# Modulation rows of the first feed-forward stage tied behind evacuations and handed out by products done

## The chip, the core and the metric

The kernel runs on one core of a Trainium2 chip. The metric is the device time of one execution in microseconds, the median of three runs. Engines are named as in the profile: PE is TensorE (matrix products; PEld are its weight loads), DVE is VectorE, ACT is ScalarE, POOL is GpSimd, and SP is the engine whose queue starts most of the DMA transfers. Every engine runs its own instructions strictly in the order in which they stand in its queue.

## What is computed

Two transformer layers run one after the other on 512 tokens of width 1024. The first ends with a feed-forward block; the second begins by scaling and shifting its input with a modulation vector that depends on nothing but the input `c`. Cut to that:

```python
# end of the first layer (D_FF = 2816)
h2 = rms_norm(x, g_ffn)
x = x + (silu(h2 @ w_gate) * (h2 @ w_up)) @ w_down
# second layer
mod = silu(c) @ w_mod + b_mod                  # 1024 x 6144 matrix, one vector of 6 * 1024
sh1, sc1, g1, sh2, sc2, g2 = split(mod, 6)
h = _rms(x, norm1_w) * (1 + sc1) + sh1
...                                            # projections, S5 scan, windowed attention, x += g1 * (...)
h2 = _rms(x, norm2_w) * (1 + sc2) + sh2
x = x + g2 * conv_ffn(h2)                      # second feed-forward block, same sizes
```

Everything is float32; a matrix product is made of three products of a high and a low part (high by high, high by low, low by high).

## The kernel before

**Products.** Each weight piece of 1024 x 128 (512 KB) is loaded as `raw` on SP's queue (two buffers). ACT copies it into `whi`, and DVE subtracts to get `wlo` (`whi` and `wlo` have five buffers each). A piece feeds 24 products of 128x512, three for each of eight slices. In the second feed-forward block `wlo` is made by ACT and an accumulating DMA on POOL's queue instead (`w8`), for the up weights.

**The feed-forward stages.** `ffn` runs over six chunks of hidden blocks (2, 4, 4, 4, 4, 4 blocks of 128). `up(c)` makes each hidden block from 48 products into two PSUM banks. In the first stage `hidden1` evacuates them: DVE writes `fg` from the gate bank, ACT applies silu, DVE writes `fu` from the up bank, multiplies, and `split` writes `hd`, the high part on ACT and the low part on DVE. `down(c)` makes eight output blocks from 3 products for each hidden block of the chunk, so 6 or 12, and DVE adds each bank into `x` (`down1`). The order is up(0), up(1), down(0), up(2), down(1), and so on; that is 1056 products for the hidden blocks and 528 for the outputs. The banks of the first stage come from a ring of three called `acc`. The last four output blocks are done apart, by halves of 256 tokens (`norm_tail`), and then `start_u` needs the modulation vector to begin the second layer.

**The modulation.** `modulation` makes the vector in rows of 128 numbers: 40 rows in the first feed-forward stage (`modT`), 8 in the second (`modG`). A row is two transfers of 256 KB into `wm` (three buffers, SP's queue) and two vector products on DVE (`CUSTOM_DVE_ANT_0` in the trace, `ISA wm,mh<-wm,cb` in the order; each is followed by a short read of the accumulator into `mh`). It is a generator: `ffn` calls `after()` behind every hidden block and every output block, `fill` then lets each of its two generators run one step further, and a row takes one or two such steps by turns. The other generator, `s5_tables`, makes tables for the second layer on DVE and POOL, with a few products and transposes on PE.

**What sets the order.** The code gives the order in which instructions are traced; a scheduler then orders each engine's queue and may move an instruction ahead of those traced before it, as soon as its operands and buffers would be there by the scheduler's own estimate. What a queue's head waits for holds everything behind it.

Of the kernel before, what the change touches and what calls it, by code (L numbers as in the profile page):

```python
# [38 lines left out]
B2 = 1  # L39
# [18 lines left out]
QK = 12  # L58
ORDER1 = "K0 TA KX0 K1 KX1 Q0 A0 QX0 Q1 dq0 A1 dq1 B QX1 QX2 CC QX3 ns00 ns01 dk0 dqx0 CD CS CT pq0 dkx0 ns10 dv0 dv1 dv2 ns11 dv3 ns20 nv00 nv01 nv10 ns30 nv11 ns21 nv20 dk1 dqx1 ns31 dkx1 nv21 nv30 TD ds0 nv31 pk0 pq1 ds1 ds2 dw0 ds3 dw1 dw2 F0 pv0 F1 pv1 dw3 F6 ss12 pv2 ss01 ss00 pv3 pk1 ss21 c0 ss32 ss31 ss13 c1 ss02 ss23 ss03 ss20 ss11 c2 ss22 F7 ss10 sv00 sv01 sv02 sv03 sv10 ss30 sv11 sv12 sv13 sv20 sv21 c3 c4 sv22 M0 ss33 c5 sv23 M1 F2 sv30 sv31 F4 sv32 sv33 F3 F5"
MOD1 = 40  # L60
EARLY = (0, 1, 6, 7, 2, 3)
LATE = (4, 5)

# [168 lines left out]
def build(tc, I, out, PV, PVN, CS, CSN, CS1, CSN1):  # L232
# [263 lines left out]

    def split(dst, src):
        act(dst[:, 0], src, AF.Copy)
        V.tensor_tensor(dst[:, 1], src, dst.bitcast(F32)[:, 0], op=ALU.subtract)  # L499

    def rsqrt_(o, ms, scale=1.0):

# [550 lines left out]
    d_x = dpool.tile([KD, P, S], F32, name="d_x")  # L1053
    d_z = [dpool.tile([8, 16, 8, 64], F32, name=f"d_z{q}") for q in range(4)]

    modG = cpool.tile([P, 8], F32, name="modG")

    def modulation(pool, j0, j1, dst, wait):

        n_ = j1 - j0  # L1060
        cb = pool.tile([P, D], F32, name="cb")
        nc.sync.dma_start(cb, I["cbc"])
        act(cb, cb, AF.Silu)
        mh = pool.tile([P, 2, n_], F32, name="mh")
        yield
        for j in range(n_):
            for n in range(2):
                wm = pool.tile([P, 512], F32, tag="wm", bufs=3, name="wm")
                nc.sync.dma_start(wm, I["wmod"][j0 + j][:, n * 512:(n + 1) * 512])
                V.tensor_tensor_reduce(wm, wm, cb[:, n * 512:(n + 1) * 512], 1.0, 0.0, ALU.mult, ALU.add, mh[:, n, j:j + 1])  # L1070
            for _ in range(wait(j)):
                yield
        V.tensor_tensor(dst, mh[:, 0], mh[:, 1], op=ALU.add)
        V.tensor_tensor(dst, dst, V1("b_mod")[:, j0:j1], op=ALU.add)
        yield
# [153 lines left out]
            nc.gpsimd.dma_start(d_rot[q], rt.rearrange("p b g c -> p b (g c)"))  # L1229
            yield  # L1230

    fillers = [s5_tables(), modulation(s5p, 0, MOD1, modT, lambda j: 1 + j % 2)]

    def fill():
        for f in fillers:
            next(f, None)

    def ffn(wn_up, wn_down, hin, hidden, add_down, after=lambda: None, start=None, tail=None, banks=(acc,)):
        banks = itertools.cycle(banks)
        hid = {}  # L1240
        started = {} if start is None else start

        def up(c):
            r, n = FCH[c]
            for j in range(r // 2, (r + n) // 2):
                ws = weights(wn_up, 2 * j), weights(wn_up, 2 * j + 1)
                for m in range(2):
                    ps = []
                    for a in range(2):
                        p_ = started.pop((j, m, a), None)  # L1250
                        if p_ is None:
                            p_ = next(banks)()
                            proj_f(p_, ws[a], hin, m)
                        ps.append(p_)
                    hid[2 * j + m] = hidden(2 * j + m, *ps)
                    after()

        def down(c):
            r, n = FCH[c]
            last = c == len(FCH) - 1  # L1260
            for k in range(8 if not (last and tail) else 8 - TAIL):
                ps = next(banks)()
                proj_f(ps, weights(wn_down, 4 * c + k // 2), hid, k % 2, k0=r)
                add_down(k, ps, last)
                after()
            if last and tail:
                tail(lambda k, ps, cs: proj_f(ps, weights(wn_down, 4 * c + k // 2), hid, k % 2, k0=r, cs=cs), add_down)

        up(0)
        for c in range(1, len(FCH)):  # L1270
            up(c)
            down(c - 1)
        down(len(FCH) - 1)
# [32 lines left out]
    def hidden1(j, pg, pu):  # L1306
        t = ftile("fg")
        V.scalar_tensor_tensor(t, pg, -0.5, r2, op0=ALU.mult, op1=ALU.mult)
        last_silu[0] = act(t, t, AF.Silu)
        u = ftile("fu")  # L1310
        V.scalar_tensor_tensor(u, pu, -0.5, r2, op0=ALU.mult, op1=ALU.mult)
        V.tensor_tensor(u, u, t, op=ALU.mult)  # L1312
        hd = hidp.tile([P, 2, S], F32R, tag="hid", name="hd")
        split(hd, u)
        return hd

    tot = sumtile()
# [11 lines left out]
    sq7 = fp.tile([P, S], F32, name="sq7")  # L1329

    def down1(k, ps, last, cs=ALL):
        V.tensor_tensor(x[k][:, cs], x[k][:, cs], ps[:, cs], op=ALU.add)  # L1332
        if last:
            dbg(f"x3_{k}", x[k])
            nc.gpsimd.dma_start(d_x[k][:, cs], x[k][:, cs])
# [371 lines left out]
    def hidden2(j, pval, pgate):  # L1707
# [2 lines left out]
        act(b, b, AF.Silu)  # L1710
        V.tensor_tensor(a, a, b, op=ALU.mult)
        hd = hidp.tile([P, 2, S], F32R, tag="hid", name="hd")
        split(hd, a)
        return hd

    def down2(k, ps, last):
# [1 line left out]
        if last:  # L1718
            nc.sync.dma_start(out[k * P:(k + 1) * P, :], x[k])

    last8 = modulation(fp, MOD1, 48, modG, lambda j: j % 2)
    ffn("w8", "w9", h2, hidden2, down2, lambda: next(last8, None), start=started, banks=(tr, sc, acc) if B2 else (acc,))
    ff.close()
    st.close()

# [25 lines left out]
```

## Time and profile before

| What | Value |
|---|---|
| Median of three runs | 1324.84 us (1318.99 to 1326.08) |
| The profiled execution, its own time | 1322.45 us |
| Its span in the trace | 1320.6 us |
| PE busy | 1238.6 us, 94% of the span |
| PE weight loads busy | 995.6 us, 75% |
| DVE busy | 835.3 us, 63% |
| ACT busy | 553.1 us, 42% |
| POOL busy | 319.4 us, 24% |
| Mean DMA rate | 146 GB/s |

PE is the busiest engine, so a change is worth what it takes from PE's idle time or from products done at a low clock. The first feed-forward stage lies at about 315 to 712 us of the span, the second from about 945 us to the end. The granted clock of PE is given in a trace as a share of full speed, 2.4 GHz; the lower of its two levels is half of that.

### The profile page before, as it was taken

What the parts mean: (1) busy time and instruction counts of PE and PEld (TensorE: products, weight loads), DVE (VectorE), ACT (ScalarE), POOL (GpSimd) and SP (SyncE); (2) the same over time, 40 slices, a digit from 0 to 9 for tenths busy, and PEclk for the clock granted to TensorE, in tenths of its full rate; (3) what the DMA queues carried; (4) which work ended last, traced back from release to release, by engine and by line L of the source; (5) the groups of instructions that cost most, each with busy time, mean ns of one, the idle gap of its engine ahead of it and who ended that gap; (6) DMA issues with size and microseconds to landing.
All of it is one profiled execution on the core that took longest, in us unless ns stands there. A gap on an engine that the chain in (4) does not pass through costs nothing.

```text
span 1320.6 us, 17314 instructions
## 1 busy us (share of the span) xinstructions
PE 1238.6 (94%) x6269; PEld 995.6 (75%) x6269; DVE 835.3 (63%) x1617; ACT 553.1 (42%) x917; POOL 319.4 (24%) x403
## 2 busy tenths in 40 slices
PE   6999999999988979999999977979889999999998
PEld 5888765667867758888888977758867788888887
DVE  7667868777977988554446588665746353434362
ACT  5434466445212213232233334665645544444430
POOL 3000004012417439391411142023121312121200
PEclk9999999999998999999999997789989999999999
DMA  6531111126567675534435883367498979595921
GB/s 214 147 118 48 49 32 49 48 80 197 152 214 221 215 243 156 160 121 126 132 105 177 274 195 103 99 162 139 97 224 187 225 161 189 126 192 120 192 88 64
DMA packets 211014, 192.96 MB, mean 146 GB/s; under 512 B 13041, under 2 KB 173697, under 8 KB 210929
## 3 DMA queue, kind: packets, MB, share of 16 engines
q1 hardware_dynamic: 154384, 146.96, 36.7%
q0 software_dynamic: 51456, 40.61, 19.3%
q10 hardware_dynamic: 5088, 4.29, 1.0%
q8 instruction: 50, 0.82, 0.3%
q14 instruction: 36, 0.29, 0.1%
HBM read 178.22 MB, written 15.43 MB: 147 GB/s over the span
## 4 chain that ended last, share of the span: by engine, by line
PE 56%; DVE 10%; DMA 8%; issue 5%; ACT 2%; POOL 1%; SPq 0%; DVEq 0%; POOLq 0%; ACTq 0%
PE acc L260 37%; PE sc L260 10%; PE tr L260 8%; DMA wm<-in_wmod_dram 4%; DVE wm L1070 2%; DMA wlo<-in_w_dram 2%; DMA raw<-in_w_dram 2%; DVE wlo L372 2%; PE po L260 1%; PE tr L1600 0%; POOL wlo L370 0%; DVE fu L1312 0%; ACT whi L366 0%; DVE x L1332 0%; DVE hd L499 0%
## 5 line engine op out<-in xcount | busy, mean ns | idle before, releaser
L260 PE MATMUL acc<-hl,whi 128*128 128x512 f32 (+1 forms) x1624 | 485.6, 382 | 15.9 <-ACT whi L366 7.5
L260 PEld LDWEIGHTS acc<-hl,whi 128*128 128x128 f32 x1624 | 296.2, 190 | 83.6 <-issue 14.0
L366 ACT ACTIVATE whi<-raw 128x1024 fp32r<-128x1024 f32 (+1 forms) x187 | 194.0, 1039 | 378.0 <-PE acc L260 193.9
L260 PE MATMUL acc<-hl,wlo 128*128 128x512 f32 (+1 forms) x812 | 309.0, 381 | 1.0 <-DMA wlo<-in_w_dram 1.0
L372 DVE TENSOR_TENSOR wlo<-raw,whi 128x1024 fp32r<-128x1024 f32 (+1 forms) x133 | 174.1, 1311 | 62.1 <-ACT whi L366 59.3
L260 PEld LDWEIGHTS acc<-hl,wlo 128*128 128x128 f32 x812 | 153.6, 189 | 33.7 <-issue 3.2
L260 PE MATMUL acc<-hd,whi 128*128 128x512 f32 (+1 forms) x472 | 147.8, 396 | 17.1 <-DVE x L1332 9.4
L370 POOL DMA_DIRECT2D wlo<-in_w_dram x54 | 72.0, 1334 | 328.1 <-ACT wlo L369 240.7
L260 PEld LDWEIGHTS acc<-hd,whi 128*128 128x128 f32 x472 | 88.7, 193 | 40.3 <-DVE x L1332 9.6
L260 PE MATMUL acc<-whi,hl 128*128 128x256 f32 (+1 forms) x544 | 111.4, 296 | 3.8 <-DVE v L249 2.2
L1070 DVE CUSTOM_DVE_ANT_0 wm<-wm,cb 128x512 f32<-128x512 f32 x96 | 79.8, 846 | 49.3 <-DMA wm<-in_wmod_dram 42.5
L260 PEld LDWEIGHTS acc<-whi,hl 128*128 128x128 f32 x544 | 91.2, 200 | 8.6 <-ACT tok L247 3.0
L260 PE MATMUL acc<-hd,wlo 128*128 128x512 f32 (+1 forms) x236 | 93.1, 394 | 0.0
L260 PE MATMUL acc<-wlo,hl 128*128 128x256 f32 (+1 forms) x272 | 80.0, 294 | 0.5 <-DVE wlo L372 0.5
L260 PE MATMUL tr<-hl,whi 128*128 128x512 f32 (+1 forms) x240 | 74.1, 392 | 0.0
L260 PE MATMUL sc<-hl,whi 128*128 128x512 f32 x208 | 64.9, 393 | 0.0
L369 ACT ACTIVATE wlo<-raw 128x1024 fp32r<-128x1024 f32 x54 | 56.5, 1046 | 3.9 <-PE acc L260 2.0
L260 PEld LDWEIGHTS acc<-wlo,hl 128*128 128x128 f32 x272 | 54.3, 200 | 2.5 <-DVE wlo L372 1.0
L919 POOL TENSOR_SCALAR_AFFINE_SELECT keep<-keep 128x128 f32<-128x128 f32 x16 | 9.3, 596 | 186.6 <-ACT keep L913 185.8
L260 PE MATMUL tr<-hl,wlo 128*128 128x512 f32 (+1 forms) x120 | 47.2, 394 | 7.4 <-DMA wlo<-in_w_dram 7.4
L260 PEld LDWEIGHTS acc<-hd,wlo 128*128 128x128 f32 x236 | 45.6, 193 | 10.0
L1332 DVE TENSOR_TENSOR x<-x,acc 128x512 f32<-128x512 f32 (+1 forms) x49 | 32.0, 655 | 33.0 <-PE acc L260 33.0
(424 smaller groups left out, 1960.1 us busy)
## 6 DMA issues: line engine op xcount, KB each, us to landing
raw<-in_w_dram SPq DMA_DIRECT2D x177, 512.0 KB, 4.4
wlo<-in_w_dram POOLq DMA_DIRECT2D x54, 512.0 KB, 8.0
wm<-in_wmod_dram SPq DMA_DIRECT2D x96, 256.0 KB, 4.1
xk<-in_xT_dram SPq DMA_DIRECT2D x16, 256.0 KB, 4.9
d_g<-s5g POOLq DMA_DIRECT2D x4, 576.0 KB, 4.1
gt<-d_g SPq DMA_DIRECT2D x4, 576.0 KB, 5.4
w1c<-in_w1k_dram SPq DMA_DIRECT2D x8, 256.0 KB, 5.7
w1c<-in_w1v_dram SPq DMA_DIRECT2D x8, 256.0 KB, 6.1
```

Of the source, the lines that this page charges most:

```text
L260: nc.tensor.matmul(o, lhsT=l, rhs=r, start=start, stop=stop, **k)
L366: act(hi[:, :m], raw[:, :m], AF.Copy)
L369: act(lo[:, :m], raw[:, :m], AF.Copy, scale=-1.0)
L370: nc.gpsimd.dma_start(v(lo), self.src[:, k0:k1, c0:c1], accum_op=ALU.add)
L372: V.tensor_tensor(lo[:, :m], raw[:, :m], hi.bitcast(F32)[:, :m], op=ALU.subtract)
L919: G.affine_select(g[:, d], g[:, d], fill=1.0, **past)
L1070: V.tensor_tensor_reduce(wm, wm, cb[:, n * 512:(n + 1) * 512], 1.0, 0.0, ALU.mult, ALU.add, mh[:, n, j:j + 1])
L1332: V.tensor_tensor(x[k][:, cs], x[k][:, cs], ps[:, cs], op=ALU.add)
```

## The change

Three things change in how the modulation rows are handed out.

- Each vector product is traced inside `tc.issue_after(done[0].ins)`. It must then stand behind that instruction in DVE's queue. `done[0]` is the last evacuation step traced so far: the DVE half of `split` for a hidden block (`hidden1`, `hidden2`), or the addition into `x` (`down1`). The tie is an order within one queue and makes no semaphore. The `wm` transfers are not tied.
- `fill` counts products. A hidden block adds 48 and an output block `3 * n`, times `MOD_RATE` = 0.0275; a whole credit runs the modulation one step. So a row comes every 36 products. `s5_tables` still gets one step for each call.
- In the second stage the eight rows are handed out at two steps for each call, instead of two rows for every two calls.

```diff
+MOD_RATE = 0.0275
...
-        V.tensor_tensor(dst[:, 1], src, dst.bitcast(F32)[:, 0], op=ALU.subtract)
+        return V.tensor_tensor(dst[:, 1], src, dst.bitcast(F32)[:, 0], op=ALU.subtract)
...
+    done = [None]
...
-                V.tensor_tensor_reduce(wm, wm, cb[:, n * 512:(n + 1) * 512], 1.0, 0.0, ALU.mult, ALU.add, mh[:, n, j:j + 1])
-            for _ in range(wait(j)):
-                yield
+                with tc.issue_after(done[0].ins) if done[0] is not None else nullcontext():
+                    V.tensor_tensor_reduce(wm, wm, cb[:, n * 512:(n + 1) * 512], 1.0, 0.0, ALU.mult, ALU.add, mh[:, n, j:j + 1])
+            yield
...
-    fillers = [s5_tables(), modulation(s5p, 0, MOD1, modT, lambda j: 1 + j % 2)]
+    fillers = [s5_tables(), modulation(s5p, 0, MOD1, modT)]
+    credit = [1.0]
 
-    def fill():
-        for f in fillers:
-            next(f, None)
+    def fill(products):
+
+        next(fillers[0], None)
+        credit[0] += products * MOD_RATE
+        while credit[0] >= 1.0:
+            credit[0] -= 1.0
+            next(fillers[1], None)
...
-                    after()
+                    after(6 * KD)
...
-                after()
+                after(3 * n)
...
-        split(hd, u)
+        done[0] = split(hd, u)
...
-        V.tensor_tensor(x[k][:, cs], x[k][:, cs], ps[:, cs], op=ALU.add)
+        done[0] = V.tensor_tensor(x[k][:, cs], x[k][:, cs], ps[:, cs], op=ALU.add)
...
-        split(hd, a)
+        done[0] = split(hd, a)
...
-    last8 = modulation(fp, MOD1, 48, modG, lambda j: j % 2)
-    ffn("w8", "w9", h2, hidden2, down2, lambda: next(last8, None), start=started, banks=(tr, sc, acc) if B2 else (acc,))
+    last8 = modulation(fp, MOD1, 48, modG)
+    ffn("w8", "w9", h2, hidden2, down2, lambda n: (next(last8, None), next(last8, None)), start=started, banks=(tr, sc, acc) if B2 else (acc,))
```

PE's order is the same in both kernels. DVE's queue in the first stage, from the `fu` of the fifth hidden block to the `fg` of the sixth, before (`fg`, `fu` read PSUM banks and so free them; `ISA` is a vector product of a modulation row):

```order
L1311 SCALAR_TENSOR_TENSOR fu<-acc,r_3100 128x512
L372 TENSOR_TENSOR wlo<-raw,whi 128x512
L1312 TENSOR_TENSOR fu<-fu,fg 128x512
L1070 ISA wm,mh<-wm,cb 128x512
L1070 ISA mh 128x1
L1070 ISA wm,mh<-wm,cb 128x512
L1070 ISA mh 128x1
L499 TENSOR_TENSOR hd<-fu,hd 128x512
L1070 ISA wm,mh<-wm,cb 128x512
L1070 ISA mh 128x1
L1308 SCALAR_TENSOR_TENSOR fg<-acc,r_3100 128x512
```

The same place in the changed kernel, up to the `fu` of the sixth block:

```order
L1318 SCALAR_TENSOR_TENSOR fu<-acc,r_3100 128x512
L373 TENSOR_TENSOR wlo<-raw,whi 128x512
L1319 TENSOR_TENSOR fu<-fu,fg 128x512
L500 TENSOR_TENSOR hd<-fu,hd 128x512
L1073 ISA wm,mh<-wm,cb 128x512
L1073 ISA mh 128x1
L1073 ISA wm,mh<-wm,cb 128x512
L1073 ISA mh 128x1
L1315 SCALAR_TENSOR_TENSOR fg<-acc,r_3100 128x512
L373 TENSOR_TENSOR wlo<-raw,whi 128x512
L1318 SCALAR_TENSOR_TENSOR fu<-acc,r_3100 128x512
```

The vector products between `fu` and `hd` are gone, and those that are left stand behind `hd`. Between the `hd` of the fourth, fifth and sixth hidden blocks there were eight and five vector products; now there are four and three, and the rest are spread behind the evacuations up to the 22nd hidden block.

SP's queue in the first stage, from the loading of `cb`, before:

```order
L1062 DMA cb<-in_cbc_dram 128x1024
L1069 DMA wm<-in_wmod_dram 128x512 x2
L1160 DMA s5bc<-in_s5bc_dram 128x4x128
L1069 DMA wm<-in_wmod_dram 128x512 x3
L354 DMA raw<-in_w_dram 128x8x128 x2
L1069 DMA wm<-in_wmod_dram 128x512 x3
L354 DMA raw<-in_w_dram 128x8x128 x2
```

And in the changed kernel:

```order
L1064 DMA cb<-in_cbc_dram 128x1024
L1071 DMA wm<-in_wmod_dram 128x512 x3
L1162 DMA s5bc<-in_s5bc_dram 128x4x128
L355 DMA raw<-in_w_dram 128x8x128
L1071 DMA wm<-in_wmod_dram 128x512 x2
L355 DMA raw<-in_w_dram 128x8x128 x3
L1071 DMA wm<-in_wmod_dram 128x512 x2
```

Eight row transfers stood ahead of the third weight load, now five; the row transfers go on until the last chunk.

DVE's queue at the start of the second feed-forward stage, before (`cf` reads a bank and is the convolution; `hl` is the last step of the stage ahead):

```order
L1351 SCALAR_TENSOR_TENSOR hl<-hm,modT,hl 128x256 x2
L1070 ISA wm,mh<-wm,cb 128x512
L1070 ISA mh 128x1
L1070 ISA wm,mh<-wm,cb 128x512
L1070 ISA mh 128x1
L1703 SCALAR_TENSOR_TENSOR cf<-acc,pv,cf 128x511 x2
L1703 SCALAR_TENSOR_TENSOR cf<-acc,pv,cf 128x510 x2
```

And in the changed kernel:

```order
L1358 SCALAR_TENSOR_TENSOR hl<-hm,modT,hl 128x256 x2
L1710 SCALAR_TENSOR_TENSOR cf<-acc,pv,cf 128x511 x2
L1710 SCALAR_TENSOR_TENSOR cf<-acc,pv,cf 128x510 x2
L1710 SCALAR_TENSOR_TENSOR cf<-acc,pv,cf 128x511
L1710 SCALAR_TENSOR_TENSOR cf<-acc,pv,cf 128x510
L1718 TENSOR_TENSOR cf<-cf 128x512
L1710 SCALAR_TENSOR_TENSOR cf<-tr,pv,cf 128x511
L500 TENSOR_TENSOR hd<-cf,hd 128x512
L1073 ISA wm,mh<-wm,cb 128x512
```

The first evacuations no longer stand behind the products of row 0; those stand behind the `hd` of the first hidden block.

## Rows read from the trace of the kernel before

**Rows 1.** Busy time by stretch of the first feed-forward stage, all engines.

```profile
core 0: us, PE busy (x) PEld busy (x) DVE busy (x) ACT busy (x) POOL busy (x), PEclk, DMA share, GB/s
315.00:375.00 60.00, 57.97 (x248) 46.16 (x247) 55.23 (x171) 20.37 (x29) 17.97 (x15) 1.00 0.54 170
375.00:495.00 120.00, 100.07 (x409) 77.20 (x408) 96.00 (x170) 28.38 (x38) 53.01 (x77) 0.93 0.73 227
495.00:615.00 120.00, 120.00 (x549) 96.75 (x548) 72.75 (x90) 36.33 (x48) 71.55 (x104) 1.00 0.47 142
```

**Rows 2.** The same stretches, DVE's instructions on the modulation rows alone.

```profile
375.00:495.00 120.00, 50.45 (x54) 0.93 0.73 227
495.00:615.00 120.00, 6.33 (x8) 1.00 0.47 142
```

**Rows 3.** What PE waited for, 315 to 500 us: total, times, longest.

```profile
PE acc L260 <- DVE x L1332: 9.4, 6, 4.2
PE acc L260 <- DVE fu L1311: 6.1, 3, 2.8
PE acc L260 <- DVE fg L1308: 4.4, 2, 2.5
```

**Rows 4.** DVE in order of time, one stall: start, length, instruction, [idle before].

```profile
393.07 0.68 DVE L1311 SCALAR_TENSOR_TENSOR fu<-acc,r 128x512 f32<-128x512 f32 x1
396.38 2.13 DVE L1070 CUSTOM_DVE_ANT_0 wm<-wm,cb 128x512 f32<-128x512 f32 x1 [2.62 <-DMA wm<-in_wmod_dram]
...
399.05 0.67 DVE L1332 TENSOR_TENSOR x<-x,acc 128x512 f32<-128x512 f32 x1
```

**Rows 5.** PE in order of time: first `hd` product, small products, a stall, the tail.

```profile
384.74 0.70 PE L260 MATMUL acc<-hd,whi 128*128 128x512 f32 x2
...
391.62 1.31 PE L1187 MATMUL tr<-cst,s5e 128*128 128x128 f32 x8
...
399.77 0.80 PE L260 MATMUL acc<-hd,whi 128*128 128x512 f32 x1 [4.24 <-DVE x L1332]
...
408.29 0.63 PE L260 MATMUL sc<-s5g,bb 128*16 128x128 f32 x16
...
710.55 0.40 PE L260 MATMUL acc<-hd,whi 128*128 128x256 f32 x2
```

**Rows 6.** A piece of the chain of waits: start, length, what.

```profile
495.97 55.76 PE acc L260 x240
```

**Rows 7.** Tile `wm`, whole program: its vector products (ns min/median/max), time to landing.

```profile
L1070 DVE CUSTOM_DVE_ANT_0 wm<-wm,cb x96: 672/691/4346, 325.9 to 1002.8; 128x512 f32<-128x512 f32 x96
DMA to landing us min/median/max: 2.5/4.1/11.8
```

**Rows 8.** Modulation products by stretch, 318 to 496 us and 496 to 700 us.

```profile
L1070 DVE CUSTOM_DVE_ANT_0 wm<-wm,cb 128x512 f32<-128x512 f32 x72 | 62.6, 885 | 23.5 <-DMA wm<-in_wmod_dram 22.4 <-ACT cb L1063 1.0
...
L1070 DVE CUSTOM_DVE_ANT_0 wm<-wm,cb 128x512 f32<-128x512 f32 x8 | 6.3, 809 | 4.9 <-DMA wm<-in_wmod_dram 4.9
```

**Rows 9.** DVE's longest modulation product, and POOL beside it, in order of time.

```profile
438.28 4.35 DVE L1070 CUSTOM_DVE_ANT_0 wm<-wm,cb 128x512 f32<-128x512 f32 x1
...
439.58 2.48 POOL L1181 TENSOR_TENSOR s5e<-s5e,s5e 128x1024 f32<-128x1024 f32 x1
```

**Rows 10.** When the modulation vector was complete (ns, start).

```profile
L1073 DVE TENSOR_TENSOR modT<-mh x1: 395/395/395, 511.2 to 511.2; 128x40 f32<-128x40 f32 x1
```

**Rows 11.** Start of the second feed-forward stage: busy time by stretch, PE's longest wait.

```profile
940.00:960.00 20.00, 15.03 (x127) 14.60 (x125) 14.10 (x34) 14.90 (x23) 2.87 (x2) 0.97 0.60 133
960.00:985.00 25.00, 23.34 (x93) 18.92 (x94) 9.93 (x22) 12.37 (x16) 5.87 (x5) 0.89 1.17 228
985.00:1000.00 15.00, 12.83 (x53) 9.54 (x52) 6.05 (x14) 3.54 (x6) 2.77 (x2) 1.00 1.25 244
1000.00:1030.00 30.00, 29.57 (x127) 23.50 (x126) 22.51 (x38) 17.65 (x24) 5.74 (x4) 1.00 0.86 171
...
961.66 0.76 PE L260 MATMUL tr<-hl,wlo 128*128 128x512 f32 x1 [6.63 <-DMA wlo<-in_w_dram]
```

More of the change, by code (lines that the diff above doesn't have):

```diff
@@ L1054, in build, with modulation @@
     d_z = [dpool.tile([8, 16, 8, 64], F32, name=f"d_z{q}") for q in range(4)]
+    done = [None]
     modG = cpool.tile([P, 8], F32, name="modG")
-    def modulation(pool, j0, j1, dst, wait):
+    def modulation(pool, j0, j1, dst):
         n_ = j1 - j0
@@ L1230, in s5_tables, with ffn @@
             yield
-    fillers = [s5_tables(), modulation(s5p, 0, MOD1, modT, lambda j: 1 + j % 2)]
-    def fill():
-        for f in fillers:
-            next(f, None)
-    def ffn(wn_up, wn_down, hin, hidden, add_down, after=lambda: None, start=None, tail=None, banks=(acc,)):
+    fillers = [s5_tables(), modulation(s5p, 0, MOD1, modT)]
[6 more added lines that the diff above has]
+            next(fillers[1], None)
+    def ffn(wn_up, wn_down, hin, hidden, add_down, after, start=None, tail=None, banks=(acc,)):
         banks = itertools.cycle(banks)
```

## The prediction

> **What bounds the kernel now.** I read the busy time by stretch first, to find where PE, the busiest engine, is not busy. In the first feed-forward stage PE works without a gap from 495 to 615 us at a granted clock of 1.00, but from 375 to 495 us it is busy for 100.07 of 120 us, at a mean clock of 0.93 [rows 1]. The reader should see two things there: 19.93 us of idle time, and a loss by the clock of at most 0.07 x 120 = 8.4 us. The same stretches for the modulation rows alone show what differs: 54 DVE instructions on them, 50.45 us, in the bad stretch, and 8 in the good one [rows 2]. (A vector product and its accumulator read count as two.)
>
> The waits say who is late. PE's idle time there ends on DVE: 9.4 us on the additions into `x`, 6.1 on `fu`, 4.4 on `fg`, in 11 waits, together 19.9 us [rows 3]. These are the instructions that free PSUM banks, and they are late because they stand behind a modulation product. One stall in order of time shows it: after `fu` at 393.07 the next DVE instruction is a modulation product that sits 2.62 us until its transfer has landed and then takes 2.13 us, so the addition into `x` starts at 399.05 [rows 4], and PE, out of banks for 4.24 us, goes on at 399.77 [rows 5]. The transfers land in 4.1 us at the median and there are three buffers [rows 7], so a run of products with nothing between them goes at the pace of the transfers: 72 products stand between 318 and 496 us, with 22.4 us of DVE idle on their transfers [rows 8].
>
> **The loss, counted a second way.** From the first product that reads `hd`, at 384.74, to the first half-width product of the tail, at 710.55, 325.8 us pass [rows 5]. Six hidden blocks are done by then (288 products) and the last four output blocks are left (48), so 1584 - 288 - 48 = 1248 products lie between. At 55.76 / 240 = 0.232 us, the pace where nothing waits [rows 6], they take 289.9 us. The small products for the tables, four groups of each of the two kinds, add about 4 x (1.31 + 0.63) = 7.8 us, an estimate from one group of each [rows 5]. That leaves 325.8 - 297.7 = 28.1 us, and idle time plus clock gave 28.3. About 1.7 of the 2.03 us of idle time between 315 and 375 us [rows 1] I count to the same cause, an estimate. So 30 us can be had here.
>
> **The change, part by part.**
> *The tie.* No instruction is added and no semaphore; a product only stands later in DVE's queue. By the order shown with the change, no product stands between `fu` and `hd` any more. What is now queued behind a product is the next `fg`, `wlo` or `x`. PE fills the bank of the next `fg` with 24 products, 5.6 us at 0.232, while it has a third bank; a pair of products takes 2 x 0.69 us [rows 7], and a landing of 4.1 us before them still ends in about that time. So a product may wait one landing there and PE does not see it. The good stretch is evidence that this cover is enough: after 496 us eight products run with 4.9 us of DVE idle on their transfers [rows 8], and PE's idle is zero [rows 1]. If the cover is gone, a wait costs PE what the 11 waits cost now, 19.9 / 11 = 1.8 us each.
>
> *The credits.* A row comes every 1 / 0.0275 = 36 products, 8.4 us; its two transfers then ask for 512 KB in 8.4 us, some 62 GB/s, beside the 142 GB/s of a stretch that had few of them [rows 1]. About 204 GB/s is below the 227 that the bad stretch moved. Three buffers cover a row and a half, 12.6 us, against the worst landing of 11.8 us [rows 7]. DVE has room: it was busy for 72.75 of 120 us in the good stretch [rows 1], and 120 / 8.4 = 14 rows there are 28 products of 0.885 us [rows 8], some 25 us instead of 6.33. SP's queue: a row's transfer waits for the product three before it, and weight loads stand behind it. In the changed order no weight load of this stage stands behind a row transfer that waits for a later DVE instruction than the weight load itself does for its own buffer, so the queue adds no wait that the buffers do not impose. I take 2 us as what is left of the 30, between 0 (the good stretch) and 14 (half of the waits stay, below): -28.
>
> *The end of the vector.* It was complete at 511 us, 199 us ahead of the tail [rows 5, 10]. Now its last step is handed out after 41 / 0.0275 = 1491 products with 45 to go before the tail, some 10 us. That cover is thin but enough for a pair of products and one landing; 0 us, and at most one median landing, 4 us, if it is gone.
>
> *The second feed-forward stage.* PE loses 4.97 + 1.66 + 2.17 + 0.43 = 9.2 us of idle time between 940 and 1030 us, and 0.03 x 20 + 0.11 x 25 = 3.4 us by the clock; the longest wait, 6.63 us, ends on the transfer of a weight's low part, not on DVE [rows 11]. By SP's order three row transfers still go out ahead of these weight loads, and the next two move from behind the second of them to behind the fourth. The bytes of eight rows still compete with weights where the DMA share is over 1. Bounds: -9 (no wait left) and +5 (row transfers now held until `hd`, with weight loads behind them, one further landing). I take -2, near the nothing that the unchanged bytes suggest.
>
> *Tables.* `s5_tables` keeps its steps. PE reaches the four groups of transposes earlier, since it waits less; the first group of small products comes 408.29 - 392.93 = 15.4 us after its transposes now [rows 5], and 30 products at 0.232 stand between them, 7 us, against two POOL instructions that I put at 2.5 us each, after the one in [rows 9]. It fits, with about 2 us to spare: 0.
>
> **Sum.** -28 - 2 = -30 us against the profiled execution's 1322.45: 1292.5. That execution lies 2.4 us under the median of the runs, within their spread of 7; I say 1293.
>
> **A rule that speaks against it.** A modulation product beside POOL's large instructions took up to 4.35 us against 0.69 [rows 7, 9]; the mean was 0.885 over 72 of them [rows 8]. The Trainium skill, in "SBUF — State Buffer", section "Who interferes with whom", says that a DVE instruction with two SBUF inputs and a GpSimd instruction that reads SBUF exclude each other for a whole instruction; the trace agrees by those rows. By the rule alone, with every product behind a large POOL instruction, the sum would be the second rival's; by the measured mean it is the one above. Spreading the products sets more of them beside POOL, which is busy for 71.55 of 120 us in the good stretch [rows 1]. DVE would be full there if a product took (120 - 66.4) / 28 = 1.9 us on average; it is a rival below.
>
> **The rivals.**
> *Half of it stays* (1308). A fourth product behind one `hd`, in the blocks that get two rows, needs the buffer that the first one frees and waits a landing with `fu` behind it. If half of the waits stay, 15 of the 30 us come back: 1322.45 - 15 = 1307.5. For it: by DVE's order four of the 22 blocks have such fours. Against: the fourth stands behind `fg`, which waits for PE longer than a landing.
> *POOL takes it* (1320). At 2.5 us a product, DVE would need 66 + 70 us in 120, 16 too many, and two such stretches eat the 30 us. Against: it needs almost three times the measured mean.
> *More than that* (1285). The rows also leave the second stage's waits: a further 7 us or so. Against: the longest wait is for weights.
> *Slower* (1330). The rows become a chain of their own: 80 products in rounds of three buffers are 27 rounds, each a landing and, as an estimate, 1 us for the product and the issue. At the median landing that is 138 us in a stage of 356 (386 less 30). It decides when the mean landing exceeds 356 / 27 - 1 = 12.2 us: then the vector is late, `start_u` waits for it, and each further microsecond costs 27 us. The time is back at 1322 at 13.3 us and at 1330 at 13.6. The worst landing was 11.8 us at 227 GB/s [rows 1, 7], which speaks against it.
>
> **How the numbers follow.** Chances: as summed 0.70 (1287 to 1300), half 0.12, more 0.08, POOL 0.06, slower 0.04. The range of 8 in 10 takes in the first and most of the second, and the third: 1285 to 1309. A measurement can tell about 0.5% here, 6.6 us. Faster by more: 0.70 + 0.12 + 0.08 = 0.90; within it: 0.06; slower: 0.04.
>
> **What would show it.** Right: PE busy for nearly all of every stretch from 315 to the tail, at a clock of 1.00, with the tail beginning near 681 us; no PE wait on `fu`, `fg` or `x` of more than a microsecond; modulation products to the end of the stage, with the vector complete some 10 us ahead of the tail. Wrong: PE waits on the same instructions at other places (half), products of 2 us and more from 480 to 620 us (POOL), `hl` of the next stage waiting for the vector (slower), or no 6 us wait for a low part near 930 us (more).

## The result, and the profile after

The changed kernel takes 1291.01 us (median of four runs, 1290.49 to 1292.43); the kernel before, run beside it on the same chip, 1321.91 us. The ratio is 0.977 (0.974 to 0.979), 31 us less. The forecast was 1293 us, between 1285 and 1309. The profiled execution of after has a span of 1288.8 us, 31.8 less than before's.

Busy time by stretch of the first feed-forward stage, the answer to [rows 1] (PE, PEld, DVE, ACT, POOL, then the granted clock, the DMA share and GB/s):

```profile
315.00:375.00 60.00, 59.45 (x256) 47.58 (x255) 54.97 (x162) 22.18 (x31) 16.48 (x15) 1.00 0.48 145
375.00:495.00 120.00, 117.88 (x543) 94.61 (x542) 92.26 (x124) 36.94 (x49) 78.16 (x115) 1.00 0.63 193
495.00:615.00 120.00, 120.00 (x541) 97.25 (x540) 84.68 (x126) 34.03 (x43) 62.45 (x104) 1.00 0.63 197
```

PE has 2.1 us of idle time left from 375 to 495 us, where it had 19.9, and its clock stays at full speed, where the mean was 0.93. The rows are now spread: DVE's instructions on them alone, the answer to [rows 2]:

```profile
315.00:375.00 60.00, 6.95 (x10) 1.00 0.48 145
375.00:495.00 120.00, 24.47 (x26) 1.00 0.63 193
495.00:615.00 120.00, 24.59 (x30) 1.00 0.63 197
615.00:682.00 67.00, 9.07 (x14) 1.00 0.52 161
```

What PE waited for from 315 to 500 us, the answer to [rows 3]: the waits for `fu` and `fg` are gone, and two short ones for `x` are left.

```profile
PE acc L261 <- DVE x L1339: 2.1, 2, 1.2
PE sc L261 <- DVE sqsum L1007: 0.6, 1, 0.6
```

PE in order of time, the answer to [rows 5]: the first product that reads `hd`, the transposes, the two stalls, the small products, the tail.

```profile
383.96 0.63 PE L261 MATMUL acc<-hd,whi 128*128 128x512 f32 x2
...
386.77 1.03 PE L1189 MATMUL tr<-cst,s5e 128*128 128x128 f32 x8
...
391.50 0.70 PE L261 MATMUL acc<-hd,whi 128*128 128x512 f32 x2 [0.91 <-DVE x L1339]
...
395.70 0.71 PE L261 MATMUL acc<-hd,whi 128*128 128x512 f32 x2 [1.21 <-DVE x L1339]
...
397.27 0.63 PE L261 MATMUL sc<-s5g,bb 128*16 128x128 f32 x16
...
682.17 0.40 PE L261 MATMUL acc<-hd,whi 128*128 128x256 f32 x2
```

From the first `hd` product to the tail 298.2 us pass now, where it was 325.8; the prediction had put the time without any loss at 297.7.

DVE in order of time, the place of [rows 4]. No product waits for its transfer here, but two of the three that follow `hd` are slow (2.75 and 1.94 us), the additions into `x` after them come late, and PE stops for 0.91 and 1.21 us in place of 4.24:

```profile
386.77 0.69 DVE L500 TENSOR_TENSOR hd<-fu,hd 128x512 fp32r<-128x512 f32 x1
387.38 0.68 DVE L1073 CUSTOM_DVE_ANT_0 wm<-wm,cb 128x512 f32<-128x512 f32 x1
...
387.99 2.75 DVE L1073 CUSTOM_DVE_ANT_0 wm<-wm,cb 128x512 f32<-128x512 f32 x1
...
390.67 1.27 DVE L1339 TENSOR_TENSOR x<-x,acc 128x512 f32<-128x512 f32 x2
391.87 1.94 DVE L1073 CUSTOM_DVE_ANT_0 wm<-wm,cb 128x512 f32<-128x512 f32 x1
```

Beside them run two large instructions of POOL, and each slow product ends some 0.5 us after one of them (which end at 390.20 and 393.26):

```profile
387.89 2.31 POOL L1200 TENSOR_TENSOR s5g<-s5bc,pw_r 128x1152 f32<-128x1152 f32 x1 [37.54 <-PE tr L1189]
390.27 2.99 POOL L1202 TENSOR_TENSOR s5g<-s5g,s5e 128x1152 f32<-128x1152 f32 x1
```

Tile `wm` over the whole program (the answer to [rows 7]) and the vector's completion (to [rows 10]):

```profile
L1073 DVE CUSTOM_DVE_ANT_0 wm<-wm,cb x96: 675/685/3161, 332.7 to 983.3; 128x512 f32<-128x512 f32 x96
DMA to landing us min/median/max: 2.6/4.0/9.1
L1075 DVE TENSOR_TENSOR modT<-mh x1: 191/191/191, 669.2 to 669.2; 128x40 f32<-128x40 f32 x1
```

The transfers land as before, and the vector is complete 13 us ahead of the tail. The first 40 rows' products together, 315 to 682 us, the answer to [rows 8] (busy, mean ns, idle time before them):

```profile
L1073 DVE CUSTOM_DVE_ANT_0 wm<-wm,cb 128x512 f32<-128x512 f32 x80 | 65.1, 844 | 3.5 <-DMA wm<-in_wmod_dram 3.5
```

They waited 3.5 us for transfers in all, where it was 27.3.

The start of the second feed-forward stage: the 90 us that answer to the four stretches of [rows 11], before and then after, and PE's longest wait after.

```profile
940.00:1030.00 90.00, 80.77 (x398) 66.56 (x397) 52.60 (x106) 48.46 (x66) 17.24 (x12) 0.96 0.95 191
```

```profile
907.00:997.00 90.00, 81.46 (x395) 67.77 (x394) 52.04 (x106) 48.30 (x66) 15.81 (x11) 0.94 0.94 191
...
927.58 0.76 PE L261 MATMUL tr<-hl,wlo 128*128 128x512 f32 x1 [5.79 <-DMA wlo<-in_w_dram]
```

Nothing was gained there: 0.7 us more of busy time at a mean clock that is 0.02 lower.

**Where the 31.8 us of the two traces lie.** I compared the start of the same matrix product in both. Across the first feed-forward stage after gains 29.5 us, all of it by 492 us of before's time; in the stages between, which the change does not touch, 4.9 us; in the second feed-forward stage it loses 1.4; and it began the first stage 1.1 us late: 29.5 + 4.9 - 1.4 - 1.1 = 31.9. The 4.9 us are not the change's. They are many small shifts. A kernel with the change in its first stage (e3_ffn1_only, below) shows 0 to 1.2 us there, by the product at which the part is taken to end, and one that gains nothing in the first stage (e1_no_tie) shows 5.2. The second stage varies as well: e3_ffn1_only, which hands out its rows there as the kernel before, is 3.2 us shorter there than before's trace. The clock has a part in it: the same products between the two stages take 219.3 us at a mean granted clock of 0.92 in e5_six_buffers and 228.1 us at 0.88 in e2_tie_only. But before (228.0) and after (223.2) both show 0.90, so the rest stays open.

### The profile page after: what moved, and what is told of

It reads as the page before. It is cut to its first block, busy times and chain, and to the rows that moved or that the text cites. A ratio compares the mean times of both kernels' runs of the same rounds, so it can differ in the third digit from the quotient of the medians.

```text
span 1288.8 us, 17279 instructions
## 1 busy us (share of the span) xinstructions
PE 1229.4 (95%) x6269; PEld 993.2 (77%) x6269; DVE 839.0 (65%) x1617; ACT 553.6 (43%) x917; POOL 319.7 (25%) x403
## 3 DMA queue, kind: packets, MB, share of 16 engines
q0 software_dynamic: 51456, 40.61, 19.8%
## 4 chain that ended last, share of the span: by engine, by line
PE 68%; DVE 6%; issue 3%; DMA 3%; ACT 2%; POOL 1%; POOLq 0%; ACTq 0%; DVEq 0%
PE acc L261 48%; PE sc L261 10%; PE tr L261 8%; DMA wlo<-in_w_dram 2%; DMA raw<-in_w_dram 1%; PE po L261 1%; PE tr L1607 1%; DVE z L1469 1%; DVE wlo L373 1%; DVE z L1458 1%; DVE z L1457 1%; DVE wm L1073 0%; POOL wlo L371 0%; ACT prob L1596 0%; PE tr L932 0%
## 5 line engine op out<-in xcount | busy, mean ns | idle before, releaser
L261 PE MATMUL acc<-hd,whi 128*128 128x512 f32 (+1 forms) x472 | 143.1, 386 | 2.1 <-DVE x L1339 2.1
L261 PEld LDWEIGHTS acc<-hd,whi 128*128 128x128 f32 x472 | 86.9, 188 | 21.7 <-issue 3.1
L1073 DVE CUSTOM_DVE_ANT_0 wm<-wm,cb 128x512 f32<-128x512 f32 x96 | 75.5, 818 | 12.1 <-DMA wm<-in_wmod_dram 12.1
L261 PEld LDWEIGHTS tr<-hl,whi 128*128 128x128 f32 x240 | 46.3, 196 | 10.3
```

Source lines behind the costliest of these rows:

```text
L261: nc.tensor.matmul(o, lhsT=l, rhs=r, start=start, stop=stop, **k)
```

## The experiments

Twelve kernels, each timed beside the kernel before. One table holds what they show of the crowded stretch, 375 to 495 us. "Work" is DVE's busy time, "waiting" its idle time ahead of modulation products that ends on their transfers, "PE" PE's busy time of the 120 us. "Returned" is what the first feed-forward stage gives back against before's trace, by the starts of the same first and last product. Times are medians, with the ratio to before, run beside it, and its 95% interval. All but the times comes from one trace of each kernel.

| Kernel | Work + waiting | PE | Returned | Median, ratio |
|---|---|---|---|---|
| before | 96.0 + 21.7 = 117.7 | 100.1 | 0 | |
| e1_no_tie | 97.8 + 18.7 = 116.5 | 97.4 | -0.7 | 1322.32, 1.000 (0.997 to 1.003) |
| e2_tie_only | 96.9 + 5.2 = 102.1 | 117.1 | 27.5 | 1296.17, 0.981 (0.975 to 0.987) |
| e3_ffn1_only | 92.8 + 1.2 = 94.0 | 117.9 | 29.6 | 1290.07, 0.976 (0.972 to 0.980) |
| changed kernel | 92.3 + 1.5 = 93.8 | 117.9 | 29.5 | 1291.01, 0.977 (0.974 to 0.979) |
| e4_no_transfer | 106.9 + 0 | 109.1 | 10.5 | 1306.65, 0.990 (0.987 to 0.994) |
| e5_six_buffers | 104.4 + 4.5 = 108.9 | 104.9 | 6.8 | 1311.88, 0.992 (0.989 to 0.995) |
| rate_0550 | 101.7 + 12.9 = 114.6 | 107.1 | 12.6 | 1307.66, 0.990 (0.988 to 0.992) |
| r0550_no_transfer | 104.6 + 0 | 112.2 | 17.5 | 1298.94, 0.984 (0.982 to 0.987) |
| rate_1100 | 105.5 + 10.7 = 116.2 | 98.0 | -2.9 | 1323.06, 1.002 (0.999 to 1.004) |
| rate_0200 | 91.4 + 0 | 118.5 | 29.2 | 1316.39, 0.995 (0.994 to 0.997) |
| a6_one_buffer | 81.1 + 37.3 = 118.4 | 111.4 | 8.1 | 1340.85, 1.017 (1.013 to 1.020) |
| e7_all48 | 93.3 + 2.3 = 95.6 | 115.9 | 26.0 | 1296.02, 0.981 (0.978 to 0.984) |
| e8_two_rates | 93.1 + 1.8 = 94.9 | 117.9 | 29.7 | 1288.88, 0.976 (0.972 to 0.979) |

The modulation products' own lines of that stretch, from which "waiting" comes (count, busy, mean ns, then the idle time before them and what ended it): before, the changed kernel, e4_no_transfer, rate_0550, a6_one_buffer.

```profile
L1070 DVE CUSTOM_DVE_ANT_0 wm<-wm,cb 128x512 f32<-128x512 f32 x54 | 50.4, 953 | 21.8 <-DMA wm<-in_wmod_dram 21.7
```

```profile
L1073 DVE CUSTOM_DVE_ANT_0 wm<-wm,cb 128x512 f32<-128x512 f32 x26 | 24.5, 971 | 1.5 <-DMA wm<-in_wmod_dram 1.5
```

```profile
L1071 DVE CUSTOM_DVE_ANT_0 wm<-w,cb 128x512 f32<-128x512 f32 x60 | 49.9, 885 | 0.0
```

```profile
L1073 DVE CUSTOM_DVE_ANT_0 wm<-wm,cb 128x512 f32<-128x512 f32 x52 | 47.6, 941 | 13.2 <-DMA wm<-in_wmod_dram 12.9
```

```profile
L1073 DVE CUSTOM_DVE_ANT_0 wm<-wm,cb 128x512 f32<-128x512 f32 x26 | 25.0, 962 | 37.4 <-DMA wm<-in_wmod_dram 37.3
```

**The credits without the tie.**

```diff
-                with tc.issue_after(done[0].ins) if done[0] is not None else nullcontext():
+                with nullcontext():
```

> The changed kernel with its credits (0.0275 of a row for each matrix product) but without the tie to the last evacuation step. Theory (where the products stand on VectorE is what counts, and the tie alone decides that, since an untied product is taken up as soon as its buffer is free): the products crowd into the first part of FFN1 as before, and the 28 to 30 us come back: 1316 to 1322 us, with the waits of TensorE for fu, fg and x between 380 and 500 us of about 20 us, and the vector complete near 510 us. Rival (the rate at which rows are handed out spreads them, the tie is only a guard): 1291 to 1296 us, vector complete after 650 us.

1322 us, as before. What PE waited for from 315 to 690 us:

```profile
PE acc L261 <- DVE fu L1318: 11.0, 4, 4.0
PE acc L261 <- DVE x L1339: 6.3, 5, 3.3
PE acc L261 <- DVE fg L1315: 5.8, 3, 3.1
```

These are the three groups of [rows 3], 23.1 us in place of 19.9. The product counter alone does nothing: in this kernel DVE's order through the stage is nearly that of before, and the vector is complete at 507.8 us (before at 511.2), since the scheduler draws an untied product forward.

**The tie without the credits.**

```diff
...
-            yield
+            for _ in range(wait(j)):
+                yield
...
-    fillers = [s5_tables(), modulation(s5p, 0, MOD1, modT)]
+    fillers = [s5_tables(), modulation(s5p, 0, MOD1, modT, lambda j: 1 + j % 2)]
...
-        next(fillers[0], None)
-        credit[0] += products * MOD_RATE
-        while credit[0] >= 1.0:
-            credit[0] -= 1.0
-            next(fillers[1], None)
+        for f in fillers:
+            next(f, None)
...
```

The last part left out gives the second stage its old steps back.

> The changed kernel with the tie, but the rows handed out by calls as before (one row each one or two calls, in FFN2 one row each one or two calls). Theory (the tie is what counts): most of the gain stays, 1291 to 1297 us; the rows bunch in the down blocks, six to eight products between two evacuations of x, so a wait of TensorE for x of 1 to 4 us in all may appear there. Rival (the tie without the even rate leaves bunches that stop TensorE in every down block): 1302 to 1312 us, with waits for x of over 8 us.

1296.17 us, and PE waits 2.8 us for `x` in all. So the tie carries most of the gain. In the trace the stage returns 27.5 us of 29.5; the two intervals overlap, so what the credits add is small and not settled by the times. The tie does two things at once: it puts the products behind evacuations, and it spreads them, since a tied product can't be drawn forward. Here the vector is complete at 672.4 us, before at 511.2, with the same calls in the code.

**The first stage alone.**

```diff
...
-            yield
+            for _ in range(wait(j)):
+                yield
...
-        done[0] = split(hd, a)
+        split(hd, a)
...
-    last8 = modulation(fp, MOD1, 48, modG)
-    ffn("w8", "w9", h2, hidden2, down2, lambda n: (next(last8, None), next(last8, None)), start=started, banks=(tr, sc, acc) if B2 else (acc,))
+    done[0] = None
+    last8 = modulation(fp, MOD1, 48, modG, lambda j: j % 2)
+    ffn("w8", "w9", h2, hidden2, down2, lambda n: next(last8, None), start=started, banks=(tr, sc, acc) if B2 else (acc,))
```

> The changed kernel with its FFN1 as changed, but in FFN2 the last eight rows untied and handed out by calls as before. Theory (all of the gain is FFN1's, and FFN2 lost about 1 us by product count): 1289 to 1292 us, TensorE in the first 80 us of FFN2 idle as long as in the kernel before. Rival (the trace of one execution misleads, FFN2's part is worth the 2 us that were predicted): 1292 to 1295 us.

1290.07 us (1289.04 to 1291.24), within a microsecond of the changed kernel. The part of the change that is in the second stage is worth nothing that can be measured.

**The kernel before without its transfers.**

```diff
+        w0 = pool.tile([P, 512], F32, name="w0")
+        nc.sync.dma_start(w0, I["wmod"][j0][:, 0:512])
...
-                wm = pool.tile([P, 512], F32, tag="wm", bufs=3, name="wm")
-                nc.sync.dma_start(wm, I["wmod"][j0 + j][:, n * 512:(n + 1) * 512])
-                V.tensor_tensor_reduce(wm, wm, cb[:, n * 512:(n + 1) * 512], 1.0, 0.0, ALU.mult, ALU.add, mh[:, n, j:j + 1])
+                wm = pool.tile([P, 512], F32, tag="wm", bufs=2, name="wm")
+                V.tensor_tensor_reduce(wm, w0, cb[:, n * 512:(n + 1) * 512], 1.0, 0.0, ALU.mult, ALU.add, mh[:, n, j:j + 1])
```

> The kernel before, with the transfers of the modulation rows left out: each product reads one resident block instead (so the modulation vector is not the reference's), 96 products of the same size on VectorE in the order that then follows, no transfer to wait for. On VectorE up to twelve products then stand between two hd, about 12 x 0.85 = 10 us beside some 5 us of evacuations and weight parts, for 48 matrix products of 11.1 us. Theory (the loss before was waiting for transfers that had not landed): VectorE's idle time ahead of the products goes to 0, and with it most of the waits of TensorE: 1293 to 1303 us, what is left being VectorE's own time. Rival (VectorE's time in the crowd is the cause, the transfers are a symptom): 1308 to 1322 us, with waits for fu and fg as long as before.

1306.65 us lies between the two. With nothing to wait for, only 10.5 of the 29.5 us come back. PE's waits from 315 to 500 us:

```profile
PE acc L260 <- DVE fu L1312: 4.5, 2, 3.5
PE acc L260 <- DVE x L1333: 3.2, 1, 3.2
PE acc L260 <- DVE fg L1309: 3.2, 1, 3.2
```

The same three instructions are late, now behind DVE's own work. Its order is denser than before's (up to twelve products between two `hd` of one chunk, before up to eight; the vector is complete at 463.2 us, before at 511.2), so this is not a clean split of before's loss; it does show that transfers were not needed for such a loss.

**Six buffers in the kernel before** (`bufs=3` to `bufs=6`, in both stages).

> The kernel before with six buffers for the modulation blocks in place of three, its order by the scheduler then a little denser still. Theory (half of the loss is a landing of 4.4 us shared by three buffers, 1.5 us for each product where VectorE needs 0.9): with six buffers the share falls to 0.7 us, the waiting for transfers goes from 22 us to under 8 us, and the time comes near the run without transfers: 1304 to 1311 us. Rival (the queue or the memory limits the landings, not the number of buffers): 1316 to 1323 us, the idle time of VectorE ahead of the products unchanged.

1311.88 us, 0.9 us outside what the theory allowed. The waiting fell as expected (21.7 to 4.5 us), but the products move up into the stretch (61 in place of 54), DVE's work there rises by 8.4 us, and the stage returns 6.8 us only. The median's 10 us hold more than that: in the trace, 8.7 us lie between the two stages, which the buffers do not touch, and the second stage is 4.0 us longer. The Trainium skill, in "Perfetto Trace Analysis", section "Optimization Strategy", says that a gap which repeats through a stretch can mean too few buffers. Here the trace agrees for less than a quarter: by buffers 6.8 of 29.5 us of the first stage came back, the rest only by the order.

**Twice the rate, with the tie** (`MOD_RATE = 0.055`).

> The changed kernel with the tie, rows handed out twice as fast (0.055 of a row for each matrix product): four products behind each hd and six to eight beside the evacuations of x, the vector complete near the middle of FFN1 (about 500 us). Theory (a product that stands behind the evacuation and finds its buffer landed costs nothing as long as VectorE has room): 1290 to 1297 us. Rival (the density alone costs, as the run without transfers lets one think, where 13 us of the 31 stayed with nothing to wait for): 1299 to 1308 us.

A miss: 1307.66 us. The tie holds, and 16.9 us of the return are lost again, most of them in waits for `x` and `fu`:

```profile
PE acc L261 <- DVE x L1339: 7.2, 6, 1.9
PE acc L261 <- DVE fu L1318: 5.7, 3, 4.0
```

**Four times the rate** (`MOD_RATE = 0.11`).

> The changed kernel with the tie, rows handed out four times as fast (0.11 of a row for each matrix product): about ten products between two hd, as dense as in the kernel before, but each behind the last evacuation step. Theory now (two parts: waiting for transfers, and VectorE's own time where ten products of 0.9 us and 5 to 6 us of evacuations and weight parts exceed the 11.1 us of 48 matrix products): 1304 to 1320 us, waits for fu, fg and x of 10 to 20 us between 375 and 500 us. Rival (the tie protects at any density): 1290 to 1297 us.

1323.06 us: at this density the tie is worth nothing. A product that is behind one evacuation is ahead of the next. The density is above before's: the vector is complete at 483.7 us, before at 511.2. The double rate is the nearer comparison, with 52 products in the stretch against before's 54 and the vector at 525.7 us, and there the tie still returned 12.6 us.

**Twice the rate without transfers.** The edit of e4_no_transfer on rate_0550.

> The changed kernel with rows at twice the rate (0.055), and the transfers of the modulation rows left out: each product reads one resident block (so the modulation vector is not the reference's). It splits the 17 us that the double rate cost. Theory (VectorE's room: its work and its waiting for blocks together may take some 100 of the 120 us from 375 to 495 us before TensorE stops; at the double rate it was 101.7 us of work and 13.2 us of waiting, so without the waiting the room suffices): 1291 to 1298 us. Rival (the dense products' own time, with the slower products beside GpSimd, is what stops TensorE): 1303 to 1309 us.

1298.94 us, 0.9 us above the theory's range. Of the 16.7 us that the double rate cost (1307.66 - 1291.01), 8.7 go with the transfers by the medians and 7.9 stay; by the two traces of the stage 4.9 go and 12.0 stay. So the split is known only roughly. By the starts of the same products, 5.9 of the 12.0 us are lost between 400 and 430 us of before's time, near the small products for the tables ([rows 5]). From 375 to 410 us of its own time DVE works 31.98 of 35 us:

```profile
375.00:410.00 35.00, 28.86 (x133) 22.92 (x132) 31.98 (x62) 9.22 (x15) 17.57 (x33) 0.90 0.32 99
```

PE's waits in the stage (315 to 690 us) show that not all of it is an evacuation behind products: the tables (`s5g` of POOL, `s5t` of DVE) are late too.

```profile
PE acc L261 <- DVE x L1340: 3.3, 1, 3.3
PE sc L261 <- POOL s5g L1203: 2.9, 1, 2.9
PE acc L261 <- DVE s5t L1090: 2.6, 1, 2.6
```

**A slower rate** (`MOD_RATE = 0.020`).

> The changed kernel with the tie, rows handed out more slowly (0.020 of a row for each matrix product): 20 products of the first 40 rows are left at FFN1's end and stand behind it on VectorE, so the vector is late. Theory (the last step has to be done some 10 us ahead of the tail; behind it 20 products at 0.9 to 1.5 us each, the upper figure one landing of 4.4 us shared by three buffers, end 18 to 30 us after the tail's start near 682 us, while the first use of the vector is at 694 us): 8 to 20 us more than the changed kernel, 1299 to 1311 us, with TensorE idle behind the norm. Rival (the norm and the tail cover them): 1290 to 1295 us.

1316.39 us, 5 us more than allowed for. The first stage itself is as good as it gets (29.2 us returned, no waiting); then the vector is late. PE's waits from 690 to 760 us, and the vector:

```profile
PE acc L261 <- ACT hl L1357: 25.1, 1, 25.1
...
L1075 DVE TENSOR_TENSOR modT<-mh x1: 199/199/199, 718.2 to 718.2; 128x40 f32<-128x40 f32 x1
```

The 20 products left over are done 37.5 us after the tail's start (680.68 us), not the 18 to 30 that I expected: 13.6 us of products, 10.5 of waiting for transfers, 1.7 of reads, and the norm's own work among them. One wait of 25.1 us takes back nearly all that the stage gave.

**One buffer in the changed kernel** (`bufs=3` to `bufs=1`, in both stages).

> The changed kernel with one buffer for the modulation blocks in place of three: each block's transfer (4.0 us from issue to landing) starts only when the product before it is done, so that a second product behind the same hd waits on VectorE for most of it. Theory (VectorE's room: 92 us of work of the 120 from 375 to 495 us, and some 28 products, half of which wait 2 to 4 us, 30 to 50 us more, so over the 100 us that there is room for): 1300 to 1315 us, waits for fu and x return. Rival (a wait that stands right behind the last evacuation step falls into the slack and costs nothing): 1290 to 1296 us.

1340.85 us, a miss on the far side, for a reason that neither theory had. The first stage still returns 8.1 us: with the same work and waiting together as before (118 us), PE is busy for 111.4 us in place of 100.1. That fits waits that stand behind evacuations, but the products there are also half as many (26 against 54), so that it is the place alone is not shown. The rest is for the most part in the second stage, where the trace loses 19.8 us: the last eight rows come so late that PE waits for the gate `modG`:

```profile
PE acc L261 <- DVE modG L1076: 16.5, 1, 16.5
PE sc L261 <- DVE cf L1710: 5.1, 1, 5.1
```

**All 48 rows in the first stage**, `MOD_RATE = 0.033`, none in the second.

> The changed kernel with the last eight modulation rows taken into FFN1 as well (48 rows at 0.033 of a row for each matrix product), so that FFN2 has no modulation rows at all. Theory (FFN1 has room for eight rows more, 14.4 us of VectorE over its 365 us, and FFN2's start, where TensorE waits 8 us for low weight parts, gets the memory and VectorE to itself): 1283 to 1288 us. Rival (the waits there are for the weights themselves, whose transfers the rows hardly delay): 1289 to 1293 us. Second rival (2.4 products for each hd are too many in the first part of FFN1, beside the tables): 1294 to 1300 us.

1296.02 us: the second rival. PE waits for the tables once, which the changed kernel does not:

```profile
PE sc L261 <- POOL s5g L1201: 2.6, 1, 2.6
```

The stage returns 26.0 us. The 3.5 us less than the changed kernel's are lost between 400 and 430 us of before's time, near the small products for the tables; after 500 us nothing more is lost.

**All 48 rows, at two rates.**

```diff
-MOD_RATE = 0.033
+MOD_RATE = (0.0275, 0.036)
+MOD_SWITCH = 672
...
+    seen = [0]
...
-        credit[0] += products * MOD_RATE
+        credit[0] += products * MOD_RATE[seen[0] >= MOD_SWITCH]
+        seen[0] += products
```

> All 48 modulation rows in FFN1 as in the run before, but at two rates: 0.0275 of a row for each matrix product for the first 672 (to some 490 us, VectorE's order there the same as in the changed kernel), then 0.036. It asks where the 5 us went that all 48 rows at one rate lost by product count between 385 and 500 us. Theory (VectorE has no room beside the tables, and has it behind them: behind 500 us the run with 0.033 lost nothing): FFN1 returns 28 to 30 us against the kernel before, FFN2's start 1 to 2 us more: 1287 to 1290 us. Rival (rows are no cheaper behind the tables, or FFN2's start depends on the weights alone): 1291 to 1296 us.

1288.88 us, in the theory's range. The stage returns 29.7 us, so the 3.5 us were lost by the rate of the first 672 products, those beside the tables. It is the lowest median of all, 2.1 us under the changed kernel, but its runs reach from 1285.08 to 1294.86 and the intervals overlap, so that it beats the changed kernel is not shown.

## Why the prediction was right, point by point

- **What bounds the kernel.** Right about the place and the instructions: the idle time and the clock of 375 to 495 us are what came back. Incomplete about the cause. The prediction named the products that wait for a transfer ahead of an evacuation. The runs show two costs of the same place: waiting, and DVE's own time where products crowd (e4_no_transfer, r0550_no_transfer). In the table, where work and waiting together stay at 102 of 120 us or below, PE is idle for at most 4.1 us; from 104.6 on it is idle for 7.8 and more. These are readings of single traces, and the sum alone does not order the kernels above that: with about 118 us PE is busy for 100.1 us in before and for 111.4 in a6_one_buffer. One reading was wrong: the 54 and 8 of [rows 2] are vector products alone (two for each row), without the accumulator reads, which add 0.08 us each; no term of the sum hangs on it.
- **Place or spreading.** The prediction had one term for both. How much of the gain comes from the place behind an evacuation and how much from the spreading is not shown, since no run spreads the products and leaves them ahead of evacuations. The nearest pair is before and rate_0550, with 54 and 52 products in the stretch: 12.6 us came back there, and the other 16.9 us only with the slower rate.
- **The loss counted by products.** Right: 298.2 us from the first `hd` product to the tail against 297.7 worked out.
- **The tie.** -28 was said and -29.5 measured. The 2 us set aside were hardly needed. One sign was missed by little: PE waits for `x` once for 1.21 us, where no wait of more than a microsecond was to be left. And one product of the 80 still stands between `fu` and `hd`, at 386.16 us, behind an addition into `x`. The cover that it claimed behind an evacuation exists, but not in full: with one buffer, 41 products waited 53.4 us from 495 to 680 us, 1.3 us each, and PE waited 8.3 us for DVE from 495 to 720 us.
- **The credits.** Their room was rightly worked out. DVE's work from 495 to 615 us is 84.7 of 120 us, where the prediction's numbers give 72.75 - 6.33 + 25 = 91 (24.6 us of products, as said, but less of the other work in that window), and the DMA rate is 197 GB/s, where 204 was said. That the rate would matter by itself is not what the prediction claimed, and e1_no_tie shows that it does not without the tie; e7_all48 and rate_0550 show that with it, it must not be much higher.
- **The end of the vector.** Right: complete 13 us ahead of the tail, where 10 were said. rate_0200 shows that this is the condition on which all rests: with 20 products behind it the price is 25 us.
- **The second stage.** -2 was said. By the trace it is +1.4, by the run without that part nothing; the traces of this stage differ by more than that without a change to it (3.2 us in e3_ffn1_only). The 5.79 us wait for a low part is where it was.
- **Tables.** Right: the first small products come 9.5 us after their transposes' end, where it was 15.4, without a wait of PE for POOL. The spare time was thin, as e7_all48 shows.
- **The sum.** 30 us were said, 31 measured. The two terms' errors, 1.5 more and 2 to 3 less, nearly cancel; the difference of the two traces holds 4.9 us of the stages between, which no term had. The term of the first stage was right by its mechanism; that the total came so close is in part luck.
- **The rivals.** *Half of it stays* and *more than that* did not come. *POOL takes it*: the products' mean is 971 ns from 375 to 495 us and the longest 3161, far from the 1.9 us at which DVE would be full. The Trainium skill's rule in "SBUF — State Buffer", section "Who interferes with whom", is borne out by single products (2.75 us beside POOL's 2.31, against 0.68 for the one ahead of it). The mean of 971 ns is far from the 2.5 us that the prediction put for a product that meets one each time. *Slower* was not reached, but its two mechanisms are real: a late vector (rate_0200) and a row held by the product before it (a6_one_buffer, 1341 us).

## What to carry over

Background work with transfers of its own goes behind the instruction that frees the foreground's buffers, and the order must be pinned: a rate at which the code hands it out has no effect if a scheduler may draw it forward. Then the density must leave the engine room, counted as work plus waiting in the tightest stretch: in these traces PE was idle for at most 4.1 us as long as that was up to 102 of 120 us. And the last piece must be done before its reader needs it. Of the four rates tried for the 40 rows, the one that ended just ahead of the reader was the best; the slower one gave the stage no more (29.2 us against 29.5) and then made the reader wait.

## What was not expected

That the crowd costs PE so much without any transfer: 19 of 29.5 us, though with products that stand closer than before's. And that the untouched stages between the two feed-forward blocks differ by up to 8.7 us (e5_six_buffers) between traces of nearly the same instructions there, more than a quarter of the effect studied.
